# First chunk's gated product transposed two steps later in FFNs 1 to 3; 512-column matmuls in the last three chunks of FFN 0

## The chip, the cores and the metric

The kernel runs on one core of one Trainium2 chip. The time is device microseconds (us) of that core, measured over whole executions. A profile of one execution by the hardware profiler gives the rows that are quoted below. The engines are PE (matrix unit, with PEld for its weight loads), DVE (vector), ACT (scalar), POOL (GpSimd) and SP, whose queue issues most of the DMA transfers.

## What is computed

Two layers of three sub-layers each, on 256 positions of width 1024: an FFN, a mixer, an FFN. Each sub-layer adds its output to the scaled input and normalises.

```python
def _swiglu(x, w_in, w_out):
    gate, up = jnp.split(x @ w_in, 2, axis=-1)
    return (jax.nn.silu(gate) * up) @ w_out
...
    for i in range(DEPTH):
        h = _layernorm(DN_ALPHA * h + 0.5 * _swiglu(h, ffn_w_in[i, 0], ffn_w_out[i, 0]), ln_g[i, 0], ln_b[i, 0])
        ...
        h = _layernorm(DN_ALPHA * h + mix, ln_g[i, 1], ln_b[i, 1])
        h = _layernorm(DN_ALPHA * h + 0.5 * _swiglu(h, ffn_w_in[i, 1], ffn_w_out[i, 1]), ln_g[i, 2], ln_b[i, 2])
```

The mixer of layer 0 is a diagonal state-space model (S5) with a gate, that of layer 1 a gated MLP (gMLP). The hidden width of an FFN is 2816, so `w_in` is 1024 x 5632 and `w_out` is 2816 x 1024. All is float32.

## The kernel before, in words

The four FFNs are called 0 to 3 here, in their order; the S5 mixer stands between 0 and 1, the gMLP mixer between 2 and 3. The instruction streams are written out by hand: each engine runs its instructions in the order in which the program issues them, and waits at the head of its queue.

**Precision.** Each float32 operand is split into a part `hi` (rounded to the matrix unit's format) and a rest `lo`. A product takes three matmuls: hi x hi, hi x lo, lo x hi (`mm3`, L200).

**Weights.** Class `Stream` (L42) loads weights in blocks of 128 x 2048 (1 MB) into three `raw` buffers, and splits each into one of five pairs `hi`, `lo`: ACT writes `hi` (L88), DVE writes `lo` (L89). The blocks are numbered through the program. A call of `tick` (L130) writes out the `lo` of the block before, issues a load if a `raw` buffer is free, starts the next split if a pair is free, and takes one piece of background work. In FFN 0 the background work is the preparation of the S5 tables: rows of L711 (DVE; the tile `pq` among them), L953 (ACT copies into `cm`, `bar` and `cl`) and two groups of 128 small matmuls (L1007) into PSUM tiles `kps`, which ACT copies out in L1009.

**FFN.** The hidden width goes in 11 chunks of 256, numbered 0 to 10. Chunk c needs two blocks of `w_in` and later one of `w_out`. For chunks 2 to 10 the loop at L539 runs the input product of chunk c, then `step_out` (L518) of chunk c - 2: 24 matmuls of 512 columns into the accumulators `acc`. The last three chunks' output products stand in `close` (L319), with the normalisation. Chunks 8, 9 and 10 of FFN 0 use the input blocks 22 and 23, 25 and 26, 28 and 29, and the output blocks 30, 31 and 32.

There are three forms of a chunk's input product.

- `step_in` (L402), for chunks 0 and 1 of FFNs 1 to 3: the positions are the stationary side, in two halves t. After the first four of the eight k steps (`cut`), a step with t = 1 calls `finish_g` (L384): PE transposes the gated products that are pending (L389), ACT and DVE split them into tiles `gt` (L392, L393). The order of the steps is (chunk, t) = (0, 0), (1, 0), (0, 1), (1, 1). So the step (0, 1) transposes the products of (0, 0) and (1, 0).
- `chunk_in` (L417), for all chunks of FFN 0 but the first: weights are stationary, all 256 positions are the moving side. A chunk has two halves m of 128 hidden columns and in each the two parts g (gate, up). Each part takes 8 k steps of three 256-column matmuls (L208 to L210). Gate and up of one m share one PSUM tile `ips`, so a chunk takes two. After the half, `act_t` (L463) applies silu to the gate (ACT, L467) and multiplies (DVE, L468); both read PSUM. `split_gt` (L473) then writes the two parts of `gt` (ACT L476, DVE L477).
- `chunk_in2` (L437), for chunks 2 to 10 of FFNs 1 to 3: `mm2t` (L212) takes two matmuls per k step, one of 512 columns (hi weights with hi and lo of x side by side, L216) and one of 256 columns (lo weights, L217). The result of each part is then the sum of two halves of its own PSUM tile, so a chunk takes four tiles `ips`, one for each (m, g). ACT copies one half out (L450), DVE adds the other (L451), ACT applies silu (L453), DVE multiplies (L455).

**PSUM.** The tiles `ips`, `kps` and the transposes' tiles all come from the pool `mm_p` (L166), which has four buffers taken in turn; the other four buffers of PSUM hold the accumulators. A tile whose buffer is still unread makes PE wait at its first matmul.

Of the kernel before, what the change touches and what calls it, by code (L numbers as in the profile page):

```python
# [154 lines left out]
def hybrid(ctx: ExitStack, tc: tile.TileContext, a: dict, out: bass.AP, subs=SUBS):  # L155
# [63 lines left out]
    def load_ln(li, si, eng):  # L219
        g = ln_p.tile([P, D], F32, tag="gam", name="gam")  # L220
        b = ln_p.tile([P, D], F32, tag="bet", name="bet")
        eng.dma_start(out=g, in_=a["ln_g"][li, si:si + 1, :].broadcast_to([P, D]))
        eng.dma_start(out=b, in_=a["ln_b"][li, si:si + 1, :].broadcast_to([P, D]))
        return g, b
# [45 lines left out]
    def in_mm(ids, t, ps, ks):  # L270
        for k in ks:
            wh, wl = ws.get(ids[k // 4])
            s = slice(512 * (k % 4), 512 * (k % 4) + 512)
            mm3(ps, xth[t][:, k], xtl[t][:, k], wh[:, s], wl[:, s], k == 0, k == KD - 1)

    def done(ids):
        for i in ids:
            ws.done(i)
# [95 lines left out]
    def ffn(ids, li, si, first, last):  # L374
# [9 lines left out]
        def finish_g():  # L384
            while pend:
                c, t, g = pend.pop(0)
                ps = mm_p.tile([P, 2, P], F32, tag="mm", name="tps")
                for m in range(2):
                    nc.tensor.transpose(ps[:, m], g[:, m * P:(m + 1) * P], ident)  # L389
                for m in range(2):  # L390
                    hi, lo = (new_gt(c, m)[:, j, P * t:P * t + P] for j in range(2))
                    nc.scalar.copy(hi, ps[:, m])  # L392
                    nc.vector.tensor_tensor(lo, ps[:, m], hi.bitcast(F32), op=ALU.subtract)  # L393

        def in_act(c, t, ps):
            sgg = g_p.tile([P, 2, FC], F32, tag="sgg", name="sgg")
            sg, g = sgg[:, 0], sgg[:, 1]
            nc.scalar.activation(sg, ps[:, :FC], AF.Silu)
            nc.vector.tensor_tensor(g, ps[:, FC:], sg, op=ALU.mult)
            pend.append((c, t, g))  # L400

        def step_in(c, t, mid=None, split=1):  # L402
            ps = mm_p.tile([P, 512], F32, tag="mm", name="ips")
            cut = 5 if mid else 4
            in_mm(ids["in"][c], t, ps, range(cut))
            if mid:
                mid()
            if t:
                finish_g()
            ws.tick(split)  # L410
            in_mm(ids["in"][c], t, ps, range(cut, KD))
            in_act(c, t, ps)
            if t == 1:
                done(ids["in"][c])
            ws.tick(split)
# [102 lines left out]
        def step_out(c, t):  # L518
            if c == 0:
                acc[t] = new_acc()  # L520
            for kt in range(2):
                for n in range(2):
                    mm_out(c, t, n, kt, acc[t][n])
            if t == 1:
                ws.done(ids["out"][c])
            split_gt()
            ws.tick()

        if first:
            start_in()  # L530
            ws.lazy = True
            chunk_in(1)
        else:
            step_in(0, 0, split=0)
            step_in(1, 0, lambda: make_xt(1))
            step_in(0, 1)
            step_in(1, 1)
        ws.lazy = True
        for c in range(2, NCH):  # L539
            (chunk_in if first else chunk_in2)(c)  # L540
            if c == NCH - 1:
                gb = load_ln(li, si, nc.gpsimd)
            if c < NCH - 1:
                step_out(c - 2, 0)
                step_out(c - 2, 1)
# [814 lines left out]
    with tc.manual_schedule():  # L1360
# [18 lines left out]
        for n, (kind, li, si) in enumerate(subs):  # L1379
            first, last = n == 0, n == len(subs) - 1  # L1380
            nxt = kinds[n + 1] if kind == "ffn" and not last else kind
            if nxt != "ffn":
                if stack is None:
                    stack = ExitStack()
                    if nxt == "gmlp":
                        gm = stack.enter_context(tc.tile_pool(name="gm", bufs=1))
                        par = load_gmlp(gm)
                        ws.background += [lambda: None] * 12 + [lambda: prepare_gmlp(par)]
                    else:
                        sm = stack.enter_context(tc.tile_pool(name="sm", bufs=1))  # L1390
                        qp = stack.enter_context(tc.tile_pool(name="qp", bufs=N_Q))
                        dr = stack.enter_context(tc.tile_pool(name="dr", bufs=1, space=bass.MemoryType.DRAM))
                        res = prepare_s5(sm, qp, dr)
            if kind == "s5" or kind == "gmlp":
                while ws.background:
                    ws.background.pop(0)()
            if kind == "ffn":
                ffn(plans[n], li, si, first, last)
            elif kind == "gmlp":
                gmlp(plans[n], par, gm, li, si, first, last)  # L1400
            else:
                s5(plans[n], res, qp, li, si, first, last)
            if kind != "ffn":
                stack.close()
                stack = None
# [24 lines left out]
```

## Time and profile before

| | us |
|---|---|
| median of 3 runs | 956.26 |
| lowest and highest | 956.1, 958.12 |
| the profiled execution: time | 957.04 |
| its span in the profile | 955.2 |
| PE busy | 937.7 (98% of the span) |
| DVE busy | 693.5 (73%) |
| ACT busy | 466.9 (49%) |

The profiled execution took 957.04 us, of which 955.2 us are the span between its first and its last instruction, and 1.84 us lie around that. In the rows of a timeline the first column is the start in us from the span's start, the second the length, then engine, line, operation and tiles; in brackets stands how long the engine had been idle and what ended that. Matmuls are pipelined, so what one of them costs is the distance between starts, not its length. FFN 0 runs to about 206 us, the S5 mixer to 312, FFN 1 to 499, FFN 2 to 687, the gMLP mixer to 759, FFN 3 to the end.

### The profile page before, as it was taken

The page shows a single profiled execution, that of the slowest core. Times are in us where ns is not written, and L with a number is a line of the kernel's source. Part 1 is how long each engine was busy: PE and PEld are TensorE (multiplying, and loading weights), DVE is VectorE, ACT ScalarE, POOL GpSimd, SP SyncE. Part 2 cuts the span into 40 slices and gives each one's busy share as a digit, 9 for nine tenths or more (in the row PEclk, how much of TensorE's full clock was granted, in tenths as well). Part 3 has the DMA queues.
Part 4 walks back from the last instruction along what each step waited for, and adds up shares of the span by engine and source line. Part 5 has one row for each costly group of instructions (what it writes and reads, how often), then busy time and mean ns, then how long its engine had stood idle before and what let it go on. Part 6 is the DMA issues. An engine that isn't in the chain of part 4 may idle for free.

```text
span 955.2 us, 15164 instructions
## 1 busy us (share of the span) xinstructions
PE 937.7 (98%) x6142; PEld 813.9 (85%) x6142; DVE 693.5 (73%) x930; ACT 466.9 (49%) x612; POOL 155.7 (16%) x228
## 2 busy tenths in 40 slices
PE   7999999999999999999999999999999999999996
PEld 6999999978898888888888888888889888888885
DVE  6789998787999766564677756556789867564655
ACT  5475347534334464545534645454445445545540
POOL 1878911001652000000001000000000000000000
PEclk9999999999999999999999999999999999999999
DMA  8787696858637657465557674646357467565521
GB/s 280 208 244 251 219 313 218 293 202 322 221 124 242 197 178 248 149 215 181 176 176 243 222 262 161 228 140 221 132 176 265 132 201 233 184 219 178 182 84 45
DMA packets 134038, 195.02 MB, mean 204 GB/s; under 512 B 7648, under 2 KB 104848, under 8 KB 133968
## 3 DMA queue, kind: packets, MB, share of 16 engines
q1 hardware_dynamic: 129296, 182.74, 58.1%
q0 software_dynamic: 4384, 10.92, 3.9%
q8 instruction: 48, 0.79, 0.3%
q10 hardware_dynamic: 288, 0.39, 0.1%
q14 instruction: 22, 0.18, 0.1%
HBM read 184.07 MB, written 9.96 MB: 203 GB/s over the span
## 4 chain that ended last, share of the span: by engine, by line
PE 75%; DVE 2%; ACT 1%; POOL 0%; issue 0%; DVEq 0%; POOLq 0%; ACTq 0%
PE ips L216 21%; PE ips L217 11%; PE acc L203 8%; PE acc L201 8%; PE acc L202 8%; PE ips L203 2%; PE ips L201 2%; PE ips L202 2%; PE pps L1152 2%; PE tps L187 1%; PE zps L210 1%; PE zps L209 1%; PE zps L208 1%; PE ups L203 1%; PE ups L201 1%; PE ups L202 1%
## 5 line engine op out<-in xcount | busy, mean ns | idle before, releaser
L216 PE MATMUL ips<-xt,hi 128*128 128x512 f32 x864 | 306.2, 398 | 0.0
L89 DVE TENSOR_TENSOR lo<-raw,hi 128x2048 fp32r<-128x2048 f32 x107 | 243.1, 2294 | 8.2 <-ACT hi L88 8.0
L217 PE MATMUL ips<-xt,lo 128*128 128x256 f32 x864 | 242.5, 281 | 0.0
L88 ACT CAST hi<-raw 128x2048 fp32r<-128x2048 f32 x107 | 204.3, 1912 | 43.8 <-PE acc L203 25.3
L216 PEld LDWEIGHTS ips<-xt,hi 128*128 128x128 f32 x864 | 162.3, 188 | 39.9
L217 PEld LDWEIGHTS ips<-xt,lo 128*128 128x128 f32 x864 | 163.1, 189 | 1.1
L201 PE MATMUL acc<-hi,gt 128*128 128x512 f32 x346 | 136.2, 394 | 0.5 <-ACT gt L476 0.5
L451 DVE TENSOR_TENSOR sgg<-sgg,ips 128x256 f32<-128x256 f32 x108 | 45.5, 421 | 124.5 <-ACT sgg L450 124.1
L203 PE MATMUL acc<-hi,gt 128*128 128x512 f32 x346 | 135.1, 391 | 0.0
L202 PE MATMUL acc<-lo,gt 128*128 128x512 f32 x346 | 134.9, 390 | 0.0
L229 POOL TENSOR_TENSOR rstd<-rstd,mhalf 128x1 f32<-128x1 f32 x14 | 13.3, 950 | 619.7 <-DVE rstd L228 619.7
L97 DVE TENSOR_TENSOR lo<-raw,hi 128x2048 fp32r<-128x2048 f32 (+2 forms) x52 | 89.8, 1754 | 24.8 <-ACT hi L96 24.6
L450 ACT COPY sgg<-ips 128x256 f32<-128x256 f32 x108 | 40.3, 373 | 115.7 <-PE ips L217 115.7
L210 PE MATMUL ips<-xt,lo 128*128 128x256 f32 x320 | 90.7, 284 | 2.1 <-DVE lo L89 2.1
L208 PE MATMUL ips<-xt,hi 128*128 128x256 f32 x320 | 90.8, 284 | 0.0
L209 PE MATMUL ips<-xt,hi 128*128 128x256 f32 x320 | 90.5, 283 | 0.0
L201 PEld LDWEIGHTS acc<-hi,gt 128*128 128x128 f32 x346 | 65.0, 188 | 14.7 <-ACT gt L476 1.3
L203 PEld LDWEIGHTS acc<-hi,gt 128*128 128x128 f32 x346 | 64.9, 188 | 14.7 <-DVE gt L477 0.3
L96 ACT CAST hi<-raw 128x2048 fp32r<-128x2048 f32 (+2 forms) x52 | 74.9, 1484 | 2.6 <-DMA raw<-in_ffn_w_in 2.3
L202 PEld LDWEIGHTS acc<-lo,gt 128*128 128x128 f32 x346 | 65.1, 188 | 12.4
L477 DVE TENSOR_TENSOR gt<-sgg,gt 128x256 fp32r<-128x256 f32 x74 | 32.2, 435 | 51.2 <-ACT gt L476 51.2
L476 ACT CAST gt<-sgg 128x256 fp32r<-128x256 f32 x74 | 30.0, 406 | 70.7 <-DVE sgg L468 43.6
(251 smaller groups left out, 1524.5 us busy)
## 6 DMA issues: line engine op xcount, KB each, us to landing
raw<-in_ffn_w_in SPq DMA_DIRECT2D x172, 512.0 KB, 5.2
raw<-in_ffn_w_out SPq DMA_DIRECT2D x44, 1024.0 KB, 5.1
raw<-in_g_w_in SPq DMA_DIRECT2D x8, 1024.0 KB, 5.1
rows<-w SPq DMA_DIRECT2D x8, 512.0 KB, 6.5
raw<-in_s_w_in SPq DMA_DIRECT2D x4, 1024.0 KB, 8.2
raw<-in_s_w_glu SPq DMA_DIRECT2D x4, 1024.0 KB, 5.0
w<-rows SPq DMA_DIRECT2D x8, 512.0 KB, 5.8
tc<-tc SPq DMA_DIRECT2D x16, 256.0 KB, 5.4
```

The source lines that it names most:

```text
L88: nc.scalar.copy(hi, raw)
L89: self.unfinished.append(lambda: nc.vector.tensor_tensor(lo, raw, hi.bitcast(F32), op=ALU.subtract))
L96: nc.scalar.copy(hi[:, s], raw[:, s])
L97: eng[p % len(eng)].tensor_tensor(lo[:, s], raw[:, s], hi[:, s].bitcast(F32), op=ALU.subtract)
L201: nc.tensor.matmul(ps, xh, wh, start=start, stop=False)
L202: nc.tensor.matmul(ps, xh, wl, start=False, stop=False)
L203: nc.tensor.matmul(ps, xl, wh, start=False, stop=stop)
L208: nc.tensor.matmul(ps, wh, xh, start=start, stop=False)
L209: nc.tensor.matmul(ps, wh, xl, start=False, stop=False)
L210: nc.tensor.matmul(ps, wl, xh, start=False, stop=stop)
L216: nc.tensor.matmul(both, wh, xt[:, :, :, k].rearrange("p t j c -> p j t c"), start=k == 0, stop=False)
L217: nc.tensor.matmul(ps[:, 0], wl, xt[:, :, 0, k], start=False, stop=k == KD - 1)
```

## The change

```diff
         def step_in(c, t, mid=None, split=1):
             ps = mm_p.tile([P, 512], F32, tag="mm", name="ips")
-            cut = 5 if mid else 4
+            cut = 5 if mid else 6 if (c, t) == (0, 1) else 4
             in_mm(ids["in"][c], t, ps, range(cut))
...
         for c in range(2, NCH):
-            (chunk_in if first else chunk_in2)(c)
+            (chunk_in if first and c < 8 else chunk_in2)(c)
```

The first line moves, in FFNs 1 to 3, the transposes of the products of (0, 0) and (1, 0) from behind the fourth k step of the step (0, 1) to behind the sixth. The second lets chunks 8, 9 and 10 of FFN 0 run as `chunk_in2`.

On DVE, in FFN 0 from the splitting of block 26 to that of block 29. The numbers behind the names tell tiles apart: `ips_1789` and `ips_1854` are the halves m of chunk 8, `ips_1977` is the first half of chunk 9, `pq` is background work. Before:

```order
L89 TENSOR_TENSOR lo26_1781<-raw26_1624,hi26_1780 128x2048
L468 TENSOR_TENSOR sgg_1844<-ips_1789,sgg_1844 128x256
...
L468 TENSOR_TENSOR sgg_1914<-ips_1854,sgg_1914 128x256
L477 TENSOR_TENSOR gt_1915<-sgg_1914,gt_1915 128x256
L89 TENSOR_TENSOR lo27_1919<-raw27_1753,hi27_1918 128x2048
...
L89 TENSOR_TENSOR lo28_1942<-raw28_1777,hi28_1941 128x2048
...
L89 TENSOR_TENSOR lo29_1966<-raw29_1815,hi29_1965 128x2048
L468 TENSOR_TENSOR sgg_2032<-ips_1977,sgg_2032 128x256
```

And in the change, where `ips_1790`, `ips_1816`, `ips_1844`, `ips_1875` are the four parts (m, g) of chunk 8, and `ips_1956` is the first part of chunk 9:

```order
L451 TENSOR_TENSOR sgg_1789<-sgg_1789,ips_1790 128x256
L89 TENSOR_TENSOR lo26_1781<-raw26_1624,hi26_1780 128x2048
L451 TENSOR_TENSOR sgg_1789<-sgg_1789,ips_1816 128x256
L455 TENSOR_TENSOR sgg_1789<-sgg_1789 128x256
...
L451 TENSOR_TENSOR sgg_1843<-sgg_1843,ips_1844 128x256
...
L451 TENSOR_TENSOR sgg_1843<-sgg_1843,ips_1875 128x256
...
L89 TENSOR_TENSOR lo28_1920<-raw28_1777,hi28_1919 128x2048
...
L451 TENSOR_TENSOR sgg_1955<-sgg_1955,ips_1956 128x256
L89 TENSOR_TENSOR lo29_1944<-raw29_1811,hi29_1943 128x2048
```

An add that reads PSUM now stands ahead of block 26's `lo`, one for each part of chunk 8 follows it, and the add of chunk 9's first part stands between the `lo` of blocks 28 and 29. Each chunk has four adds and two products where it had two products. The order of the other DVE work is the same.

On PE, chunks 8 and 9 of FFN 0: the first matmul on each PSUM tile of the pool of four, in turn. Before, chunk 8 has two tiles, chunk 9 has two, with the two background tiles `kps` behind the first half and inside the second:

```order
L208 MATMUL ips_1789<-xt_96,hi22_1562 128x256
...
L208 MATMUL ips_1854<-xt_96,hi22_1562 128x256
...
L208 MATMUL ips_1977<-xt_96,hi25_1755 128x256
...
L1007 MATMUL kps_2037<-cm0_1369,bar0_1634 32x64
...
L208 MATMUL ips_2103<-xt_96,hi25_1755 128x256
...
L1007 MATMUL kps_2130<-cl_1848,bar0_1634 32x32
```

In the change:

```order
L216 MATMUL ips_1790<-xt_96,hi22_1562 128x512
...
L216 MATMUL ips_1816<-xt_96,hi22_1562 128x512
...
L216 MATMUL ips_1844<-xt_96,hi22_1562 128x512
...
L216 MATMUL ips_1875<-xt_96,hi22_1562 128x512
...
L216 MATMUL ips_1956<-xt_96,hi25_1755 128x512
...
L216 MATMUL ips_1982<-xt_96,hi25_1755 128x512
...
L1007 MATMUL kps_2004<-cm0_1369,bar0_1634 32x64
...
L216 MATMUL ips_2071<-xt_96,hi25_1755 128x512
...
L1007 MATMUL kps_2093<-cl_1837,bar0_1634 32x32
...
L216 MATMUL ips_2160<-xt_96,hi25_1755 128x512
```

With four buffers taken in turn, `kps_2130` before follows on `ips_1854`, the second half of chunk 8. In the change `kps_2093` follows on `ips_1956`, the first part of chunk 9, and the last part `ips_2160` follows on a tile that the copy of `kps_2004` (L1009) frees.

On PE in FFN 1, the step (0, 1) around the moved transposes; `hi45` is the first of the chunk's two blocks (k steps 0 to 3), `hi46` the second. Before:

```order
L201 MATMUL ips_3814<-hi45_3585,xt_96 128x512
L202 MATMUL ips_3814<-lo45_3586,xt_96 128x512
L203 MATMUL ips_3814<-hi45_3585,xt_96 128x512
L389 MATMUL tps_3827<-ident_85,sgg_3762 128x128 x2
L389 MATMUL tps_3836<-ident_85,sgg_3811 128x128 x2
L201 MATMUL ips_3814<-hi46_3598,xt_96 128x512
L202 MATMUL ips_3814<-lo46_3599,xt_96 128x512
```

In the change:

```order
L203 MATMUL ips_3748<-hi45_3519,xt_96 128x512
L201 MATMUL ips_3748<-hi46_3532,xt_96 128x512
L202 MATMUL ips_3748<-lo46_3533,xt_96 128x512
L203 MATMUL ips_3748<-hi46_3532,xt_96 128x512
...
L389 MATMUL tps_3767<-ident_85,sgg_3696 128x128 x2
L389 MATMUL tps_3776<-ident_85,sgg_3745 128x128 x2
L201 MATMUL ips_3748<-hi46_3532,xt_96 128x512
```

Six matmuls of the second block now stand ahead of the four transposes. The queues of SP and POOL have the same order as before.

## The prediction

> **What bounds the kernel now.** I read the chain of waits first, then PE's waits, then the timelines of DVE, ACT and PE around chunks 8 to 10 of FFN 0. The first line is the chain that ended last, the others are what PE waited for (us in total, times, longest us).
>
> ```profile
> PE 75%; DVE 2%; ACT 1%; POOL 0%; issue 0%; DVEq 0%; POOLq 0%; ACTq 0%
> ```
> ```profile
> PE ips L210 <- DVE lo L89: 2.1, 2, 1.5
> ...
> PE tps L389 <- DVE sgg L399: 0.6, 3, 0.2
> PE acc L201 <- ACT gt L476: 0.5, 2, 0.3
> ```
>
> The kernel is PE's stream almost from end to end. So two things count: how many us of matmuls the change takes out of that stream, and whether PE comes to wait where it did not. The change touches only the last two waits directly. In FFN 0 PE runs far ahead of the other two engines, which also split the weights and prepare the S5 tables. DVE there, around chunk 8:
>
> ```profile
> 157.47 2.29 DVE L89 TENSOR_TENSOR lo<-raw,hi 128x2048 fp32r<-128x2048 f32 x1
> 159.68 0.42 DVE L468 TENSOR_TENSOR sgg<-ips,sgg 128x256 f32<-128x256 f32 x1
> ...
> 167.31 0.42 DVE L477 TENSOR_TENSOR gt<-sgg,gt 128x256 fp32r<-128x256 f32 x1 [2.68 <-ACT gt L476]
> 167.65 2.29 DVE L89 TENSOR_TENSOR lo<-raw,hi 128x2048 fp32r<-128x2048 f32 x1
> ...
> 171.78 2.29 DVE L89 TENSOR_TENSOR lo<-raw,hi 128x2048 fp32r<-128x2048 f32 x1
> ...
> 175.92 2.29 DVE L89 TENSOR_TENSOR lo<-raw,hi 128x2048 fp32r<-128x2048 f32 x1
> ```
>
> These are the `lo` of blocks 26, 27, 28 and 29. Between the last three lies background work (`pq`). And PE in chunks 9 and 10:
>
> ```profile
> 159.82 0.39 PE L210 MATMUL ips<-xt,lo 128*128 128x256 f32 x1 [0.63 <-DVE lo L89]
> ...
> 164.07 1.99 PE L1007 MATMUL kps<-cm,bar 128*32 128x64 f32 x128
> ...
> 169.07 1.30 PE L1007 MATMUL kps<-cl,bar 128*32 128x32 f32 x128
> ...
> 173.27 0.40 PE L201 MATMUL acc<-hi,gt 128*128 128x512 f32 x1
> ...
> 178.74 0.28 PE L208 MATMUL ips<-xt,hi 128*128 128x256 f32 x1
> ...
> 190.25 0.40 PE L201 MATMUL acc<-hi,gt 128*128 128x512 f32 x1
> ```
>
> The second group of `kps` ran at 169.07, and PE reached the output product of chunk 7 at 173.27, while DVE's `lo` of block 28 was still running. The lag is 6 us and more, and before the change it costs nothing, because two tiles per chunk are enough.
>
> **Matmuls of 512 columns.** Chunk 10 took 190.25 - 178.74 = 11.51 us for 32 sets (a k step of one part), 0.360 each. In FFN 1, where `chunk_in2` runs:
>
> ```profile
> 359.88 0.40 PE L216 MATMUL ips<-xt,hi 128*128 128x512 f32 x1
> ...
> 363.76 0.40 PE L216 MATMUL ips<-xt,hi 128*128 128x512 f32 x1
> ```
>
> Eleven sets lie between these two rows: 3.88 / 11 = 0.353. So a chunk saves 32 x 0.007 = 0.23 us, three chunks 0.7, if PE waits for nothing new. [...]
>
> **What the four tiles cost.** A tile of `chunk_in2` needs an ACT copy and a DVE add before its buffer is free. Their price, in groups of FFN 1 (count | busy us, mean ns):
>
> ```profile
> L451 DVE TENSOR_TENSOR sgg<-sgg,ips 128x256 f32<-128x256 f32 x32 | 13.5, 421 | 38.1 <-ACT sgg L450 38.1
> L450 ACT COPY sgg<-ips 128x256 f32<-128x256 f32 x31 | 11.6, 373 | 38.4 <-PE ips L217 38.4
> ...
> L453 ACT ACTIVATE sgg<-sgg 128x256 f32<-128x256 f32 x16 | 6.7, 419 | 7.9 <-DVE sgg L451 7.9
> ```
>
> In chunk 9 the pool's turn comes round to its first part: the second `kps` group must wait for the add of part (0, 0) of chunk 9. By DVE's order this add stands behind the `lo` of blocks 27 and 28 and the `pq` work behind each, just where the `lo` of block 29 started at 175.92. So the question is how much later DVE gets there. ACT's rows:
>
> ```profile
> 158.87 0.39 ACT L467 ACTIVATE sgg<-ips 128x256 f32<-128x256 f32 x1
> ...
> 163.79 1.91 ACT L88 CAST hi<-raw 128x2048 fp32r<-128x2048 f32 x1
> 165.60 1.25 ACT L953 COPY cl<-pq 64x512 f32<-64x512 f32 x2
> 166.87 0.41 ACT L476 CAST gt<-sgg 128x256 fp32r<-128x256 f32 x1
> ...
> 177.64 0.58 ACT L1009 COPY k<-kps 128x512 f32<-128x512 f32 x1
> ```
>
> DVE's stretch from 167.31 to 175.92, 8.61 us, begins with L477, which waits for ACT's cast at 166.87. I walk the queues with the row durations and 0.05 us per handover (my estimate; an engine starts up to 0.1 us ahead of the end of the row before it).
>
> - DVE: the add of (0, 0) goes ahead of the `lo` of block 26, which ends near 160.1; then add and product of the first half, in place of one product at 159.68; DVE is free again at 160.80 for `pq` (1.93 us: the 4.14 between the starts of two `lo`, less 2.21), then L477 (0.33), at 163.06 the add of (1, 0), `pq` until 165.33.
> - ACT: the silu of (1, 0) needs that add, so it runs 163.52 to 163.94, then a `cl` copy (1.25), the copy of (1, 1) from 165.08, block 27's `hi` from 165.40 instead of 163.79, one `cl`, and the cast at 168.42 instead of 166.87: 1.55 us later.
> - DVE: L477 moves from 167.31 to 168.86, and the add of chunk 9's first part starts 8.61 later, at 177.47, and ends at 177.90. Bounds for the shift of 1.55: 0, and 2.3 (chunk 8's four copies and two of its adds in full).
> - PE: chunk 9 cannot start until the add of chunk 8's first part is done, 157.95; at its fifth k step it waits for block 26's `lo` as before (159.82, now 160.14). Part (0, 0) ends at 161.32, (0, 1) 8 x 0.353 later at 164.15, the first `kps` group takes 2.0, part (1, 0) ends at 168.98. Then PE stands until 177.95, **9.0 us**.
> - The last part (1, 1) needs the buffer of the first `kps` group. Its copy (L1009) stands in ACT's queue behind the silu (177.95 to 178.37), a `cl` copy to 179.57 and the copy of (0, 1) to 179.89; it ends at 180.43. PE runs the second `kps` group meanwhile (1.3) and starts (1, 1) at 180.48, ending at 183.30. The row of 173.27 is so moved by **+10.03 us**.
>
> The wait is PE's, so nothing covers it, and behind it stand all of PE's later matmuls. It gives some back. Chunk 10 is 0.23 shorter; its buffers are free in time, with PE 10 us later. The two waits for `gt` in `close` go, and so does one in front of the transposes of the S5 input, because DVE and ACT have caught up:
>
> ```profile
> 192.77 0.39 PE L203 MATMUL acc<-hi,gt 128*128 128x512 f32 x1
> 193.43 0.50 PE L201 MATMUL acc<-hi,gt 128*128 128x512 f32 x1 [0.27 <-ACT gt L476]
> 193.77 0.39 PE L202 MATMUL acc<-lo,gt 128*128 128x512 f32 x1
> ...
> 206.22 1.23 PE L187 MATMUL tps<-ident,h 128*128 128x128 f32 x8 [0.35 <-DVE h L238]
> ```
>
> From 192.77 to 193.77 are 1.00 us; two undisturbed starts take 2 x 0.228 (24 matmuls between 173.27 and 178.74 took 5.47). So such a wait costs 0.54, the two 1.08, the third 0.35. FFN 0: 10.03 - 0.23 - 1.08 - 0.35 = **+8.37**.
>
> **The clock.** Nine idle us are enough to lower PE's clock. The last matmul, the granted clock behind it (columns: window, length, five engines, PEclk, DMA share, GB/s), and two matmuls at the start:
>
> ```profile
> 947.52 0.28 PE L203 MATMUL ops<-hi,gt 128*128 128x256 f32 x1
> ```
> ```profile
> 953.00:954.00 1.00, 0.00 (x0) 0.00 (x0) 0.00 (x0) 0.00 (x0) 0.00 (x0) 0.52 0.57 191
> ```
> ```profile
> 13.06 0.63 PE L201 MATMUL ips<-hi,xt 128*128 128x512 f32 x1
> ...
> 17.33 0.61 PE L202 MATMUL ips<-lo,xt 128*128 128x512 f32 x1
> ```
>
> About 5.3 us after the last matmul the granted clock was 0.52. At the start ten matmuls took 4.27 us, 0.427 each instead of 0.228, so each us at that clock loses 0.47, and it lasted at least these 4.27. That gives 2.0 us for the row's stretch, and for 3 to 6 us of low clock 1.4 to 2.8. I take **+2.2**; the lower bound is 0, if no drop comes. [...]
>
> **The moved transposes.** FFN 1, with two undisturbed transposes further on:
>
> ```profile
> 329.13 0.39 PE L203 MATMUL ips<-hi,xt 128*128 128x512 f32 x1
> ...
> 329.93 0.44 PE L389 MATMUL tps<-ident,sgg 128*128 128x128 f32 x2 [0.19 <-DVE sgg L399]
> 330.13 0.48 PE L201 MATMUL ips<-hi,xt 128*128 128x512 f32 x1
> ```
> ```profile
> 335.47 0.39 PE L203 MATMUL ips<-hi,xt 128*128 128x512 f32 x1
> ...
> 335.84 0.48 PE L201 MATMUL ips<-hi,xt 128*128 128x512 f32 x1
> ```
>
> Two transposes cost 0.37 - 0.228 = 0.14, so four should make 0.51 of the 1.00 us between 329.13 and 330.13. PE waits for the product of (1, 0) on DVE. Six matmuls ahead of them (1.37 us) put the transposes at 330.7, and the product is there at 329.9. What comes later with them, the `gt` splits on ACT and DVE, is next needed 5 us on (335.84), so nothing new waits. I take 0.45 for each of the three: **-1.35**; bounds 0.6 (the idle in the waits) and 1.47.
>
> **The sum.** 8.37 + 2.2 - 1.35 = +9.22. The profiled execution took 957.04, so 966.3; it lies 0.78 above the median, and for the median of 956.26 I forecast **965.5**.
>
> **Rivals.**
> - *The stall without a clock drop* (the idle stretch is broken by the short `kps` group, and the granted clock holds): 965.5 - 2.2 = 963.3. Against it speaks 0.52 behind the last matmul. Chance 0.17.
> - *A longer stall or slower warming*: DVE later by the other bound (2.3 instead of 1.55, +0.75) and 6 us and more of low clock (+0.6 to +1.5): about 967.5. For it speaks how tight ACT's queue is; chance 0.12.
> - *The buffers come free in time, and the kernel is faster.* If the add of chunk 9's first part ran before PE reaches the second `kps` group at 169.0, the gains would stand alone: 956.26 - 0.7 - 1.35 = 954.2. It would have to run 8.5 us ahead of my walk. Against it speaks that even without any delay DVE's row at this place starts at 175.92. Chance 0.04.
> - *Between*: the add done by about 171, a stall of 2 us that the gains just cover, 956.3. Chance 0.02.
> - *The moved transposes do nothing*, since PE merely meets another wait there: 965.5 + 1.35 = 966.9, inside my range, counted with the forecast.
>
> The forecast with its small errors has the rest, 0.65. Range: the bounds of the shift (-1.55, +0.75) and of the clock (1.4 to 2.8, and 0 with its own chance) give 962.0 to 968.5; the two fast rivals and the ends of the slow one are left out. A difference of 0.2% (1.9 us; the runs shown lie 956.1 to 958.12) is about what a measurement of this kernel can tell from none. Faster by more than that 0.04, within it 0.02, slower 0.94.
>
> **What would show it.** After the change PE should have one idle gap of 7 to 11 us in chunk 9 of FFN 0, ahead of the second `kps` group, ended by DVE's add (L451); a shorter one behind that group, ended by ACT L1009; a granted clock near 0.5 for 3 to 6 us; no wait for `gt` in `close`; and no wait at L389 for L399. I am wrong if PE has no such gap, or if the add stands elsewhere in DVE's queue in time; if the gap is there and the whole is less than 6 us slower, what comes back in FFN 0 was larger than the 1.66 us (0.23 + 1.08 + 0.35) that I took.

## The result and the profile after

The change makes the kernel slower: 965.82 us (median of 4; 965.59 to 967.45) against 956.18 (median of 4), ratio 1.0093, 95% interval 1.0078 to 1.0107. The forecast was 965.5, the range 962.0 to 968.5.

PE's waits after the change (us in total, times, longest us):

```profile
PE kps L1007 <- DVE sgg L451: 8.9, 1, 8.9
...
PE ips L216 <- DVE sgg L451: 0.8, 1, 0.8
...
PE ips L216 <- ACT k L1009: 0.5, 1, 0.5
```

These three are new. The waits at L389 (0.6 before) and for ACT's `gt` (0.5) are gone. The long one in PE's timeline, with the rows on both sides:

```profile
159.12 0.50 PE L216 MATMUL ips<-xt,hi 128*128 128x512 f32 x1 [0.78 <-DVE sgg L451]
...
170.15 0.28 PE L217 MATMUL ips<-xt,lo 128*128 128x256 f32 x1
179.36 1.93 PE L1007 MATMUL kps<-cl,bar 128*32 128x32 f32 x128 [8.93 <-DVE sgg L451]
...
181.75 0.79 PE L216 MATMUL ips<-xt,hi 128*128 128x512 f32 x1 [0.46 <-ACT k L1009]
...
186.30 0.39 PE L201 MATMUL acc<-hi,gt 128*128 128x512 f32 x1
...
191.78 0.39 PE L216 MATMUL ips<-xt,hi 128*128 128x512 f32 x1
...
203.07 0.40 PE L201 MATMUL acc<-hi,gt 128*128 128x512 f32 x1
```

PE ends the part (1, 0) of chunk 9 at 170.4 and stands until the second `kps` group at 179.36. What it waits for, in DVE's timeline:

```profile
170.19 0.43 DVE L477 TENSOR_TENSOR gt<-sgg,gt 128x256 fp32r<-128x256 f32 x1 [2.63 <-ACT gt L476]
170.54 2.28 DVE L89 TENSOR_TENSOR lo<-raw,hi 128x2048 fp32r<-128x2048 f32 x1
...
174.67 2.29 DVE L89 TENSOR_TENSOR lo<-raw,hi 128x2048 fp32r<-128x2048 f32 x1
...
178.80 0.41 DVE L451 TENSOR_TENSOR sgg<-sgg,ips 128x256 f32<-128x256 f32 x1
179.13 2.28 DVE L89 TENSOR_TENSOR lo<-raw,hi 128x2048 fp32r<-128x2048 f32 x1
```

The add of chunk 9's first part stands behind two `lo` and the background work. PE's granted clock (the column behind the five engines) falls in the gap, at 175.16 (0.58 in the window from 175 is 0.16 us at 1.00 and the rest at 0.50), and is back at 185.40, 6.0 us after PE took up work:

```profile
174.00:175.00 1.00, 0.00 (x0) 0.00 (x0) 0.96 (x3) 0.17 (x1) 0.00 (x0) 1.00 0.52 123
175.00:176.00 1.00, 0.00 (x0) 0.00 (x0) 1.00 (x1) 0.99 (x2) 0.00 (x0) 0.58 1.01 418
...
184.00:185.00 1.00, 1.00 (x5) 0.81 (x4) 0.00 (x0) 0.15 (x1) 0.56 (x1) 0.50 0.93 324
185.00:186.00 1.00, 1.00 (x7) 0.92 (x6) 0.00 (x0) 0.00 (x0) 0.55 (x2) 0.80 0.88 299
```

FFN 1's transposes stand in one row, without a wait:

```profile
342.23 0.39 PE L203 MATMUL ips<-hi,xt 128*128 128x512 f32 x1
342.46 0.60 PE L389 MATMUL tps<-ident,sgg 128*128 128x128 f32 x4
342.81 0.48 PE L201 MATMUL ips<-hi,xt 128*128 128x512 f32 x1
```

**Where the time lies.** The moment at which the input arrives differs between executions; the first L389 row stands between 29.77 and 31.85 in the profiles here. So FFN 0 is measured from its first transposes of L389 to the second group of transposes in front of the S5 mixer, in each profile. Before:

```profile
30.59 0.60 PE L389 MATMUL tps<-ident,sgg 128*128 128x128 f32 x4
```
```profile
217.52 1.03 PE L187 MATMUL tps<-ident,h 128*128 128x128 f32 x8
```

and after:

```profile
31.48 0.60 PE L389 MATMUL tps<-ident,sgg 128*128 128x128 f32 x4
```
```profile
228.51 1.03 PE L187 MATMUL tps<-ident,h 128*128 128x128 f32 x8
```

That is 186.93 before and 197.03 after: **+10.10**. The span grew from 955.2 to 965.7, by 10.5: 0.89 at the start, 10.10 in this stretch, 0.75 in the S5 mixer (94.40 to 95.15, told at the end), -1.29 from there to the last matmul (635.60 to 634.31), which is FFNs 1 to 3, and 0.05 behind it. The -1.29 is steady: this last stretch takes 634.3 us in all nine profiles with the moved transposes and 635.6 in the two without.

### The profile page after: what moved, and what is told of

The parts are those of the page before. It is cut to its first block, busy times and chain, and to the rows that moved or that the text cites. A ratio compares the mean times of both kernels' runs of the same rounds, so it can differ in the third digit from the quotient of the medians.

```text
span 965.7 us, 14998 instructions
## 1 busy us (share of the span) xinstructions
PE 937.8 (97%) x6046; PEld 810.8 (84%) x6046; DVE 698.6 (72%) x942; ACT 471.7 (49%) x624; POOL 155.6 (16%) x228
## 4 chain that ended last, share of the span: by engine, by line
PE 78%; DVE 3%; POOL 1%; ACT 0%; issue 0%; DVEq 0%; ACTq 0%; POOLq 0%
PE ips L216 22%; PE ips L217 11%; PE acc L203 8%; PE acc L201 8%; PE acc L202 8%; PE ips L201 2%; PE ips L203 2%; PE ips L202 2%; PE pps L1152 2%; PE tps L187 1%; PE zps L210 1%; PE zps L209 1%; PE zps L208 1%; PE ups L203 1%; PE ups L201 1%; PE ups L202 1%
## 5 line engine op out<-in xcount | busy, mean ns | idle before, releaser
L216 PE MATMUL ips<-xt,hi 128*128 128x512 f32 x960 | 342.0, 400 | 1.2 <-DVE sgg L451 0.8
L216 PEld LDWEIGHTS ips<-xt,hi 128*128 128x128 f32 x960 | 181.1, 189 | 46.0 <-DVE sgg L451 1.2
L217 PEld LDWEIGHTS ips<-xt,lo 128*128 128x128 f32 x960 | 182.1, 190 | 1.8 <-DVE lo L89 0.6
L451 DVE TENSOR_TENSOR sgg<-sgg,ips 128x256 f32<-128x256 f32 x120 | 50.5, 421 | 133.0 <-ACT sgg L450 132.1
L450 ACT COPY sgg<-ips 128x256 f32<-128x256 f32 x120 | 44.7, 373 | 123.3 <-PE ips L217 123.2
L477 DVE TENSOR_TENSOR gt<-sgg,gt 128x256 fp32r<-128x256 f32 x74 | 32.2, 435 | 50.9 <-ACT gt L476 50.9
L208 PE MATMUL ips<-xt,hi 128*128 128x256 f32 x224 | 63.4, 283 | 0.0
L209 PE MATMUL ips<-xt,hi 128*128 128x256 f32 x224 | 63.4, 283 | 0.0
```

What stands on the lines that cost most here:

```text
L208: nc.tensor.matmul(ps, wh, xh, start=start, stop=False)
L209: nc.tensor.matmul(ps, wh, xl, start=False, stop=False)
L216: nc.tensor.matmul(both, wh, xt[:, :, :, k].rearrange("p t j c -> p j t c"), start=k == 0, stop=False)
L217: nc.tensor.matmul(ps[:, 0], wl, xt[:, :, 0, k], start=False, stop=k == KD - 1)
```

## The experiments

Each was timed beside the kernel before on the same chip. "FFN 0" is the stretch above in the profile, against 186.93.

| run | median us | before there | ratio, 95% interval | FFN 0 |
|---|---|---|---|---|
| the change | 965.82 | 956.18 | 1.0093, 1.0078 to 1.0107 | +10.10 |
| cut_only | 956.24 | 957.67 | 0.9982, 0.997 to 0.9995 | +0.18 |
| cut_5 | 956.03 | 957.44 | 0.9983, 0.9971 to 0.9996 | -0.63 |
| chunks_only | 966.82 | 957.67 | 1.0094, 1.0074 to 1.0114 | +10.02 |
| chunk9_alone | 963.28 | 957.67 | 1.0062, 1.0042 to 1.0081 | +7.09 |
| chunks_8_10 | 957.86 | 957.67 | 1.0, 0.9989 to 1.0012 | +1.31 |
| warm_gap | 965.27 | 957.44 | 1.008, 1.0055 to 1.0105 | +8.71 |
| late_add | 968.7 | 957.44 | 1.0119, 1.0098 to 1.014 | +12.18 |
| kps_apart | 963.69 | 957.44 | 1.0071, 1.0047 to 1.0095 | +7.05 |
| kps_apart_old | 958.91 | 958.12 | 1.0004, 0.9992 to 1.0017 | +2.78 |

The FFN 0 of a run is that of one execution. The kernel before, cut_only and cut_5 have the same code there and differ by up to 0.8 us, so differences below that say nothing.

**Each part alone.** cut_only has the first line of the diff, chunks_only the second.

> Only the moved transposes; all chunks of FFN 0 as before. My theory: each of the three waits at L389 goes and gives 0.45 us, in all -1.35, so about 954.8 us. Rival (PE meets another wait there and nothing is gained): 956.2. Second rival (only the idle time that the waits listed, 0.6 in all, is gained): 955.6.

> Only the three chunks as 512-column matmuls. My theory: the stall in chunk 9 and its cold clock do not depend on the transposes, so 965.8 + 1.35 = 967.2 us, with a wait of about 8.9 us at the second kps group. Rival (the two parts work on each other): anything clearly away from 967.2.

The transposes by themselves bring 0.0018 x 957.67 = 1.7 us, interval 0.5 to 2.9, which holds both the 1.35 and the 0.6; the traces decide with 1.29 in FFNs 1 to 3, here as in the change. (In this profile the S5 mixer took back 0.75 of it, which is told at the end.) The chunks by themselves cost +9.0 by the ratio, interval +7.1 to +10.9; the +11 that I expected (967.2 against 956.2) lies just above it. Their FFN 0 is the change's within 0.1, with a wait of 8.82. So the parts do not work on each other: FFN 0 has all of the loss, and -1.7 + 9.0 = 7.3 agrees with the change's +8.9 within the intervals. In cut_only PE did not wait for `gt` in `close`, and waited 1.64 instead of 0.35 for the normalisation behind it, so such waits trade places in FFN 0 even where the code is the same.

**One step later instead of two.**

```diff
-            cut = 5 if mid else 4
+            cut = 5 if mid or (c, t) == (0, 1) else 4
```

> Only the moved transposes, one k step later instead of two (three matmuls, 0.68 us, ahead of them). My theory: the product is there 0.5 us behind the third matmul of the fourth step, so the wait goes here too: -1.35 us against before, as with two steps. Rival (the splits behind the transposes need the second step): a wait at L389 of 0.1 to 0.2 is left, and the gain is a half. In the S5 mixer a POOL operation (L1204) took 2.56 us instead of 1.43 in the profiles of the four kernels with moved transposes and of neither without, and PE waited 0.46 for it; if that hangs on the moved transposes it is here too, if on chance it may not be.

The wait is gone here too, FFNs 1 to 3 are 1.29 shorter as with two steps, and the ratio is the same. One step is enough.

**Which of the three chunks.**

```diff
-            (chunk_in if first and c < 8 else chunk_in2)(c)
+            (chunk_in if first and c != 9 else chunk_in2)(c)
```
```diff
-            (chunk_in if first and c < 8 else chunk_in2)(c)
+            (chunk_in if first and c not in (8, 10) else chunk_in2)(c)
```

> The moved transposes, and of the three chunks only chunk 9 with four tiles. My theory: the turn of the pool in chunk 9 alone makes the stall; DVE reaches the add of chunk 9's first part 1.55 us earlier, at about 175.9, so PE stands about 7.7 us, the clock still falls: about 963.5 us. Rival (the cost is the added work of ACT and DVE, in equal parts over the three chunks): a third of the loss of 10.9, so about 958.5.

> The moved transposes, and chunks 8 and 10 with four tiles, chunk 9 with two as before. My theory: no tile of chunk 9 takes a buffer of chunk 9, so no long wait and no fall of the clock; waits under 1.5 us at chunk 9's and chunk 10's first tile, most of it given back at the waits in close: about 955 us. Rival (added work of ACT and DVE): two thirds of the loss, about 962.

Chunk 9 alone makes the long wait, at the place and of the size expected:

```profile
175.78 1.93 PE L1007 MATMUL kps<-cl,bar 128*32 128x32 f32 x128 [7.44 <-DVE sgg L451]
```

It makes +7.09 of the +10.10, and by the ratio +5.9, interval +4.0 to +7.8, where I expected +7.3 and the rival +2.3. Chunks 8 and 10 make no long wait, and the rival's two thirds are refuted; but I expected 955, and the kernel is no faster than before: the 1.3 us of the transposes are eaten. The rows show two waits:

```profile
178.83 0.50 PE L216 MATMUL ips<-xt,hi 128*128 128x512 f32 x1 [0.73 <-ACT k L1009]
...
195.16 0.50 PE L201 MATMUL acc<-hi,gt 128*128 128x512 f32 x1 [1.33 <-ACT gt L476]
```

The first stands at chunk 10's first tile. The second stands in `close`, for the last `gt` of chunk 10, which here comes behind the chunk's copies and adds (L450, L451); before, PE waited there twice, 0.53 in all. So the 0.23 us that a chunk's matmuls save are saved in front of a wait.

**The clock.** warm_gap fills the gap with work that counts for nothing: part (1, 0) of chunk 9 is computed four times over, and only the last time is kept.

```diff
-                    for k in range(KD):
+                    for k in [*range(KD)] * (4 if first and (c, m, g) == (9, 1, 0) else 1):
```

> The change, with the part (1, 0) of chunk 9 of FFN 0 run four times over on the same tile (only the last time counts): 24 k-step sets more, 24 x 0.353 = 8.5 us of work for PE in the stretch where it stood 8.9 us. My theory: PE waits only 0.5 us at the second kps group, the granted clock stays at 1.0, and the last part of chunk 9 takes 2.8 us instead of 4.55: 1.7 us faster than the change, so about +7.9 against before, though PE does 8.5 us more. Rival (the stall alone is the cost, the clock costs nothing): as the change, +9.6. Rival (PE's work is what counts): +18.

```profile
179.63 1.29 PE L1007 MATMUL kps<-cl,bar 128*32 128x32 f32 x128 [0.34 <-DVE sgg L451]
...
182.02 0.50 PE L216 MATMUL ips<-xt,hi 128*128 128x512 f32 x1 [1.10 <-ACT k L1009]
```
```profile
170.00:180.00 10.00, 9.66 (x95) 8.20 (x97) 9.47 (x11) 6.11 (x9) 0.00 (x0) 1.00 0.63 191
180.00:190.00 10.00, 8.90 (x146) 7.54 (x133) 6.38 (x9) 7.59 (x12) 1.10 (x2) 1.00 1.02 344
```

The clock stays at 1.00, the `kps` group takes 1.29 instead of 1.93, and the last part of chunk 9 runs from 182.02 to 184.96, 2.94 instead of 4.55. FFN 0 is 1.39 shorter than with the change (+8.71 against +10.10), although PE does 8.5 us more. So the fall of the clock costs about 1.4 by these two profiles, and the rows of the last part show where. By the ratio the run is +7.7, interval +5.3 to +10.1; that holds the +7.9 of my theory and the rival's +9.6 alike, so here the rows decide. The rival's +18 is refuted. Of the 1.61 that the last part saves 0.24 are lost, because it starts that much later behind the copy of L1009.

**DVE's queue.** late_add lets DVE write the `lo` of block 28 twice, with the same values (its edit moves all later lines down by one).

```diff
-            self.unfinished.append(lambda: nc.vector.tensor_tensor(lo, raw, hi.bitcast(F32), op=ALU.subtract))
+            twice = 2 if self.n_split == 29 else 1
+            self.unfinished.append(lambda: [nc.vector.tensor_tensor(lo, raw, hi.bitcast(F32), op=ALU.subtract) for _ in range(twice)])
```

> The change, with DVE writing the lo of block 28 twice (the same values), 2.2 us more in DVE's queue ahead of the add of chunk 9's first part. My theory: the wait at the second kps group grows by 2.2 to about 11.1 us and the whole by as much: about +11.8 against before. Rival (the wait is set by ACT, the copies or a transfer, and DVE has room): as the change, +9.6.

```profile
179.98 1.94 PE L1008 MATMUL kps<-cl,bar 128*32 128x32 f32 x128 [11.25 <-DVE sgg L452]
```

The second `lo` takes 2.33 us more of DVE's time ahead of the add, and the wait grows from 8.93 to 11.25, by 2.32. FFN 0 grows by 2.08 and the ratio from 1.0093 to 1.0119 (the intervals overlap). DVE's queue sets the end of the wait, us for us.

**The `kps` groups elsewhere.** In kps_apart chunk 9 has four tiles of its own, and no fifth.

```diff
-        add(50, 0, k_products, 0)
-        add(51, 0, k_products, 2)
+        add(54, 0, k_products, 0)
+        add(58, 0, k_products, 2)
```

> The change, with the two kps groups due four and seven ticks later: the first behind the output product of chunk 7, the second behind the last part of chunk 10, so that chunk 9 has four tiles of its own and none of them takes a buffer of chunk 9. My theory: the first kps group takes the buffer of chunk 9's first part, at 175.3 in place of 169.0, and waits only for the 2.6 us until the add is done at 177.9; no fall of the clock; some waits under 1 us at chunk 10's tiles and the second group; 1.8 us given back at the end of FFN 0: about +0.3 against before, between -1 and +2.5. Rival (four tiles per chunk cost by the added copies and adds, wherever the kps groups stand): near +9.

This missed: +6.8 (interval +4.5 to +9.1) instead of at most +2.5. The long wait is gone, and the first group waits less than I thought; but there is a row of other waits:

```profile
173.10 0.50 PE L202 MATMUL acc<-lo,gt 128*128 128x512 f32 x1 [1.40 <-DVE lo L89]
...
179.59 1.99 PE L1007 MATMUL kps<-cm,bar 128*32 128x64 f32 x128 [0.98 <-DVE sgg L451]
...
182.03 0.50 PE L216 MATMUL ips<-xt,hi 128*128 128x512 f32 x1 [0.45 <-DVE sgg L451]
...
191.49 0.50 PE L216 MATMUL ips<-xt,hi 128*128 128x512 f32 x1 [0.72 <-ACT k L1009]
```
```profile
212.97 1.75 PE L187 MATMUL tps<-ident,h 128*128 128x128 f32 x8 [2.70 <-DVE h L238]
```

The last of them is not the tiles': DVE waits there for beta's load, whose buffer `bet` the tile `k` occupies until the second group is copied and stored. So the same edit was run with the old chunks.

> The moved transposes and the two kps groups at their later ticks, but all chunks of FFN 0 with two tiles as before: what moving the groups costs by itself. In the profile of kps_apart DVE waited 2.89 us for the load of beta (tile bet), whose buffer holds the tile k until the second group is copied and stored, and PE 2.70 behind it, with a fall of the clock. My theory: that belongs to the later groups, not to the four tiles; here the copy comes some 4 us earlier, at about 196, and beta 11.5 us behind it as there, at 208, so a wait of about 3 us is left: about +2.5 against before, and of the +6.8 of kps_apart about 4 are the four tiles'. Rival (the whole +6.8 is the four tiles'): -1.3, no wait for beta.

```profile
206.72 1.41 DVE L238 SCALAR_TENSOR_TENSOR h<-r,rstd,bet 128x512 f32<-128x512 f32 x2 [4.14 <-DMA bet<-in_ln_b]
```

The wait for beta is here too, so it belongs to the moved groups. They cost FFN 0 +2.78 in this profile. By the ratio the run is only +0.4 against before (interval -0.8 to +1.6), where I expected +2.5; that is 2.1 above cut_only. Between these two runs only the three chunks differ, and that difference is 7.05 - 2.78 = 4.3 us in the profiles and 6.8 - 0.4 = 6.4 by the ratios. So four tiles cost 4 to 6 us even where no tile of chunk 9 waits for chunk 9. The turn of the pool makes one wait of 9 us with a slow clock behind it; without the turn a part of the loss, how much beyond 4 us stays open, comes back as small waits for the same late engines. My theory named the place and the size of the wait, but its other half, that without the turn the tiles cost almost nothing, falls.

## Why the prediction was right

In each profile I take times from the first L389 row, so that the input's arrival drops out.

- **The long wait.** Forecast 9.0, measured 8.93, at the group and behind the add that were named; chunk9_alone and late_add show that DVE's queue sets its end. The shift of DVE was forecast as 1.55, bounds 0 and 2.3; L477 moved from 167.31 to 170.19, less the 0.89 of the start, 1.99. PE reached the group later as well (first tile of chunk 9 at 159.12: +0.88, forecast +0.60), so the wait itself kept its length.
- **The row of 173.27.** Forecast +10.03; it stands at 186.30, 12.14 later, of which 4.55 - 2.82 = 1.73 are the slow clock in the last part, so 10.41.
- **The clock.** Forecast +2.2, bounds 0 and 2.8; 1.73 in the trace of the change, 1.39 by warm_gap. The term was somewhat too large: the slow clock ended 6.0 us behind the gap, but the first 2.4 of them went to the second `kps` group and to the wait for the first group's copy (L1009), where it cost nothing, and only 3.65 fell on large matmuls. The rate was right, though the column stands at 1.00 at the program's start, where it was taken: matmuls of 512 columns are 0.427 apart there, and 0.43 in the change where the column reads 0.50. The 3 to 6 us of slow clock that the term was taken from were an estimate: the rows of before show only the 4.27 at the start. Measured, the clock was back 6.0 us after PE took up work (179.36 to 185.40), and 2.9 to 6.2 in the other profiles with such a fall.
- **What comes back.** Chunk 10 took 203.07 - 191.78 = 11.29 instead of 11.51: -0.22, forecast -0.23. From there to the second group at L187 it is 25.44 instead of 27.27: -1.83, forecast -1.43. The missing 0.4 is the wait for `h`, for which I took its idle time of 0.35, and not the distance between starts.
- **The moved transposes.** Forecast -1.35, measured -1.29; what came later with them, the splits into `gt`, held nobody up.
- **The sum.** 10.10 - 1.29 = 8.81 against the forecast of 9.22; the 0.75 in the S5 mixer were in no part of it, and the rest up to 9.64 is within what one execution and the median can differ. So it is in part luck that the time came within 0.4 us of the forecast: the row of 173.27 without the clock (+0.38), the clock (-0.47), what came back (-0.39), the transposes (+0.06) and the mixer (+0.75) nearly cancel.
- **The range.** Its ends do not quite follow from the bounds that it names: 965.5 + 0.75 + 0.6 is 966.9, not 968.5, and 965.5 - 1.55 - 2.2 is 961.8, not 962.0. The measured time lies within either.

The signs that the prediction named are all there: the gap, the shorter one of 0.46 behind the group, ended by L1009, the clock at 0.50, and no wait for `gt` in `close` or at L389; only the slow clock lasted longer than the 3 to 6 us named, 10.24 in all and 6.0 behind the gap. The rival without a fall of the clock is refuted by that 0.50, the rival that the moved transposes do nothing by the -1.29. The rival that the buffers come free in time had the right condition (the add done by 169.0) and is refuted by more than 9 us: the add ends at 179.2, 0.89 of it from the start.

## What to carry to other kernels

A change that takes more buffers from a pool with a fixed turn is priced by walking the turn: which instruction frees the buffer that the next tile takes, and what stands ahead of that instruction in its engine's queue. Ask of an engine that lags behind PE whether somebody needs its last result: DVE's lag of 6 us and more cost no wait at the second `kps` group before, and 8.93 us in the change, where that group needed DVE's add. Saving matmul time in front of such an engine saved nothing here, as chunks 8 and 10 show (ratio 1.0, +1.31 in FFN 0). And of this change only the first line was worth keeping, for a gain of 0.2% (ratio 0.9982, at most 0.9995), and one step later does as well as two.

## What was not expected of the hardware

PE's clock fell behind a wait of only 2.70 us. In kps_apart PE stood for 2.70 us, in kps_apart_old for 3.30, and in both the granted clock fell to 0.50, in kps_apart when PE was already at work again (at 213.40, 0.43 us after 212.97); in cut_only, with 1.64 us at the same place, it stayed at 1.00. kps_apart, from the wait on, and cut_only:

```profile
211.00:212.00 1.00, 0.00 (x0) 0.00 (x0) 0.00 (x0) 0.00 (x0) 0.00 (x0) 1.00 0.97 385
212.00:213.00 1.00, 0.03 (x1) 0.06 (x1) 0.93 (x2) 0.00 (x0) 0.00 (x0) 1.00 0.39 156
213.00:214.00 1.00, 1.00 (x6) 0.76 (x7) 1.00 (x2) 0.29 (x1) 0.00 (x0) 0.70 0.00 0
214.00:215.00 1.00, 1.00 (x6) 0.90 (x5) 0.96 (x3) 0.55 (x2) 0.00 (x0) 0.50 0.00 0
...
216.00:217.00 1.00, 1.00 (x4) 0.76 (x4) 0.06 (x1) 1.00 (x1) 0.00 (x0) 0.59 0.00 0
```
```profile
206.00:207.00 1.00, 0.41 (x4) 0.42 (x4) 1.00 (x2) 0.00 (x0) 0.00 (x0) 1.00 0.00 0
207.00:208.00 1.00, 1.00 (x8) 0.80 (x7) 0.97 (x3) 0.74 (x2) 0.00 (x0) 1.00 0.00 0
```

The slow clock lasted unequal times. In kps_apart it begins at 213.40 and ends at 216.82, if the 0.70 and 0.59 above are made up of 1.00 and 0.50; such a reading is good to about 0.02 us. Five profiles in which the clock fell in or behind a wait of PE, read in the same way (us):

| run | PE stood | clock fell, after PE stopped | slow clock lasted | back, after PE took up work |
|---|---|---|---|---|
| kps_apart | 2.70 | 3.1 | 3.42 | 3.9 |
| kps_apart_old | 3.30 | 2.8 | 3.42 | 2.9 |
| chunk9_alone | 7.44 | 4.4 | 6.82 | 3.8 |
| the change | 8.93 | 4.7 | 10.24 | 6.0 |
| late_add | 11.25 | 3.8 | 13.66 | 6.2 |

In chunks_only, behind its wait of 8.82, 512-column matmuls take 0.42 until 184.32 and 0.24 from 184.54 on, 5.8 us after PE took up work. The five slow stretches are 1, 1, 2, 3 and 4 times 3.42 us, within 0.02. So in these profiles the price of a gap did not grow evenly with it: PE stood 1.5 us less in chunk9_alone than in the change, but the slow clock was 3.42 us shorter, and the last part of chunk 9 took 3.56 us there instead of 4.55. What sets the length of the slow clock and the moment at which it begins is not shown.

In the S5 mixer one POOL operation beside two of DVE goes in one of two ways. Before, and in cut_only:

```profile
283.52 1.43 POOL L1204 TENSOR_TENSOR xt<-y,xt 128x256 fp32r<-128x256 f32 x1 [3.82 <-ACT xt L1197]
```
```profile
283.14 2.89 DVE L119 TENSOR_TENSOR lo<-raw,hi 128x1024 fp32r<-128x1024 f32 x2
```
```profile
283.90 2.56 POOL L1204 TENSOR_TENSOR xt<-y,xt 128x256 fp32r<-128x256 f32 x1 [3.81 <-ACT xt L1197]
```
```profile
283.52 2.35 DVE L119 TENSOR_TENSOR lo<-raw,hi 128x1024 fp32r<-128x1024 f32 x2
```

What POOL loses, 1.13 us, DVE gains in part, 0.54, and PE waits 0.46 for POOL: the mixer takes 95.15 instead of 94.40 us. The slow way stands in the profiles of the change and of all its relatives with moved transposes but kps_apart, and in neither kernel without them. As the moved transposes come later than the mixer, and kps_apart has them, they are not shown to be the cause; what decides is open. If they were, a good half of their 1.29 us would go back there.
